# In-projections in pieces of 512 weight columns, and gate and up products with 512 moving columns, in a four-layer decoder trunk

## The chip, the cores and the metric

The kernel runs on one core of one Trainium2 chip. The metric is the device time of one execution in microseconds (us), the median of three runs. Six actors matter below: TensorE (PE, matmuls; PEld is its weight load, which runs beside it), VectorE (DVE), ScalarE (ACT), GpSimd (POOL), and SyncE (SP), which issues the DMA transfers. TensorE has two clock levels, 1.2 and 2.4 GHz; the profile shows which share of full speed it was granted.

## The reference, cut to what matters

Four layers over 256 positions of width 1024. Each layer is a token mixer with a memory attention beside it, one output projection, a normalisation, a gated feed-forward net (FFN) of width 2816, and a second normalisation. The mixer kinds are 0, 1, 2, 0: kind 0 picks keys by an indexer before it attends, kind 1 combines three dilated groups of heads, kind 2 comes down to causal attention at this length.

```
for i in range(4):                                  # x: 256 x 1024
    q, k, v, (qi, wi, ki), qm = split(x @ w_in[i])  # 768, 768, 768, (512, 8, 64 in kind 0), 256 columns
    q, k = rope(q), rope(k)                         # first 16 of each head's 64 columns turn; qi, ki too
    if kind == 0:  sel = top_64(sum_h wi * relu(qi_h . ki)); mix = attention(q, k, v, over sel)
    if kind == 1:  o_g, l_g = dilated(q_g, k_g, v) for g in 0..2; mix = sum_g softmax(l)_g * o_g
    if kind == 2:  mix = causal_attention(q, k, v)
    mk, mv = split(layer_norm(mem) @ w_mem_kv[i])
    mo = attention(qm, mk, mv)
    x = layer_norm(ALPHA * x + concat(mix, mo) @ w_out[i])
    g, u = split(x @ w_gate_up[i])                  # 2816 columns each
    x = layer_norm(ALPHA * x + (silu(g) * u) @ w_down[i])
```

## The kernel before, in words

**Products.** Every fp32 product is made as three passes. Each operand is split into a high part (`wh`, `xh`, `fth`) and a low part, the rest (`wl`, `xl`, `ftl`), and `mm3` issues high by high, low by high and high by low (L260, L261, L262). So each tile of a product is three matmuls.

**Weights.** The weights stream through the chip once. `weight_plan` lists pieces (`v`, `qk`, `qi`, `qm`, `mk`, `mv`, `out`, `gu`, `dn`) in order of use. Each piece is a few halves of 128 x 1024 floats (512 KB): a DMA issued by SP (L210) brings one into a `raw` buffer (4 of them), ACT casts the high part (L218), and DVE (L234) or POOL (L232, two instructions of 512 columns) subtracts for the low part. POOL takes three of four halves in the mixers and none in the FFN. Six buffers hold converted pairs (`NB = 6`).

**Forms of a product.** `a_mode` keeps the activations stationary and moves the weights: for each of 8 depth blocks three matmuls of as many columns as the piece is wide, once for each half of the positions (tb 0 and tb 1). The in-projection pieces use it: six pieces `qk` (one pair of heads each, 128 columns of q and 128 of k), three `v`, and for the indexer `qi` in 328 and 256 columns. `t_mode` keeps the weights stationary and moves the activations, 256 columns (all positions). The FFN's gate and up pieces (`gu`, 22 a layer, of which the first two use `a_mode`) and `qm` use it. The down and output projections move 512 weight columns.

**A gate and up piece.** `t_mode` leaves gate and up in one PSUM bank; `t_task` then runs silu on ACT (L1025), the product with up on DVE (L1027), the high part on ACT (L1029) and the low part on DVE (L1031). The plan of the FFN alternates two `gu` pieces with one `dn` piece, which uses products of the pair of `gu` pieces before the last one done and the first of that pair.

**A pair of heads.** A `qk` bank is copied to `nat` on ACT (L469), four small DVE operations turn its first columns (`rope`, L461 to L464), PE transposes it (L477), ACT and DVE copy q and k out (L571, L572), PE makes logits (L491), DVE masks them and takes their minimum (L502), ACT exponentiates, PE transposes the result (`turned`, L526) and multiplies with v (L543), DVE scales (L547), PE transposes again (L553), and the split (L269, L274) gives `fth` and `ftl` for the output projection.

**The dilated combine.** In layer 1 `dil_combine` adds the three groups' exponentials with weights: on DVE small operations on `st` tiles (L882 to L889), two scalings (L892) and four multiply-adds per half of the positions (L894; tiles `e`, 128 x 128 for tb 0, `E`, 128 x 256 for tb 1). There are two sets of heads (jp 0, jp 1) by two halves, so four combines. Before the change, the pieces of jp 0 come first and its combines are spawned after the third of them, in the middle of the in-projections; jp 1's at the end.

**Order.** PE runs in the order in which the program is written: a small scheduler written in Python (`tick`) places the steps of waiting tasks between groups of large matmuls. The other engines are ordered by a tile scheduler by priority. The memory's normalisation (two multiply-adds of 128 x 512 per half, L350 and L352, DVE) is a low-priority task of layer 0; PE transposes its result (L326).

## Time and profile before

| | |
|---|---|
| median of 3 runs | 1340.44 us (1339.45 to 1341.69) |
| profiled execution: time | 1339.27 us |
| profiled execution: span of the instructions | 1337.5 us |
| mean granted TensorE clock | 0.995 |
| PE busy | 1305.3 us, 98% of the span |
| DVE, ACT, POOL busy | 776.9, 651.3, 313.3 us |
| weights moved | 224.10 MB, 51.2% of the DMA engines' time |

A busy time is the sum of an engine's instructions on the profile. Matmuls overlap in the pipeline, so a matmul's duration is longer than the time to the next one's start; where the pace of PE counts, starts are compared.

### The profile page before, as it was taken

What the parts mean: (1) busy time and instruction counts of PE and PEld (TensorE: products, weight loads), DVE (VectorE), ACT (ScalarE), POOL (GpSimd) and SP (SyncE); (2) the same over time, 40 slices, a digit from 0 to 9 for tenths busy, and PEclk for the clock granted to TensorE, in tenths of its full rate; (3) what the DMA queues carried; (4) which work ended last, traced back from release to release, by engine and by line L of the source; (5) the groups of instructions that cost most, each with busy time, mean ns of one, the idle gap of its engine ahead of it and who ended that gap; (6) DMA issues with size and microseconds to landing.
All of it is one profiled execution on the core that took longest, in us unless ns stands there. A gap on an engine that the chain in (4) does not pass through costs nothing.

```text
span 1337.5 us, 23972 instructions
## 1 busy us (share of the span) xinstructions
PE 1305.3 (98%) x9370; PEld 1205.4 (90%) x9370; DVE 776.9 (58%) x1660; ACT 651.3 (49%) x1216; POOL 313.3 (23%) x277
## 2 busy tenths in 40 slices
PE   7899999999999999999999999999998999999997
PEld 5799899999999799999999989999987998899996
DVE  7845465555656874555474465555576755655555
ACT  5556454444465554444456545444445654444441
POOL 3543330000353440000054442000034443300000
PEclk9999999999999999999999999999999999999999
DMA  8443365556463356555554337656544333655551
GB/s 293 162 157 112 110 231 186 185 187 188 150 214 112 111 175 219 189 183 185 177 188 137 110 118 234 187 187 189 187 155 172 127 111 111 209 187 187 188 176 62
DMA packets 63186, 225.63 MB, mean 169 GB/s; under 512 B 7776, under 2 KB 7776, under 8 KB 63072
## 3 DMA queue, kind: packets, MB, share of 16 engines
q1 hardware_dynamic: 62784, 224.10, 51.2%
q8 instruction: 73, 1.20, 0.4%
q14 instruction: 41, 0.34, 0.1%
q10 hardware_dynamic: 288, 0.00, 0.0%
HBM read 223.02 MB, written 1.05 MB: 168 GB/s over the span
## 4 chain that ended last, share of the span: by engine, by line
PE 89%; DVE 5%; issue 2%; POOL 2%; DMA 1%; ACT 1%; SPq 0%; DVEq 0%; POOLq 0%; ACTq 0%
PE bank L260 27%; PE bank L262 26%; PE bank L261 26%; PE bank L491 3%; PE bank L543 3%; POOL wl L232 2%; PE bank L526 2%; DMA raw<-in_w 1%; PE bank L477 1%; DVE wl L234 1%; PE bank L326 1%; DVE E L894 1%; PE bank L553 1%; ACT wh L218 0%; DVE e L894 0%
## 5 line engine op out<-in xcount | busy, mean ns | idle before, releaser
L218 ACT CAST wh<-raw 128x1024 fp32r<-128x1024 f32 (+1 forms) x402 | 421.0, 1048 | 366.7 <-PE bank L261 179.3
L234 DVE TENSOR_TENSOR wl<-raw,wh 128x1024 fp32r<-128x1024 f32 (+1 forms) x294 | 379.3, 1291 | 296.0 <-ACT wh L218 294.9
L232 POOL TENSOR_TENSOR wl<-raw,wh 128x512 fp32r<-128x512 f32 x216 | 293.7, 1383 | 726.5 <-ACT wh L218 690.8
L260 PE MATMUL bank<-xh,wh 128*128 128x256 f32 x1344 | 381.7, 284 | 0.0
L262 PE MATMUL bank<-xh,wl 128*128 128x256 f32 x1344 | 380.3, 283 | 0.0
L261 PE MATMUL bank<-xl,wh 128*128 128x256 f32 x1344 | 380.3, 283 | 0.0
L260 PEld LDWEIGHTS bank<-xh,wh 128*128 128x128 f32 x1344 | 257.7, 192 | 2.8 <-issue 1.3
L261 PEld LDWEIGHTS bank<-xl,wh 128*128 128x128 f32 x1344 | 257.7, 192 | 1.2
L262 PEld LDWEIGHTS bank<-xh,wl 128*128 128x128 f32 x1344 | 257.7, 192 | 0.0
L260 PE MATMUL bank<-wh,xh 128*128 128x256 f32 (+1 forms) x768 | 231.4, 301 | 1.3 <-ACT xh L269 0.9
L261 PE MATMUL bank<-wl,xh 128*128 128x256 f32 (+1 forms) x768 | 219.5, 286 | 2.2 <-DVE wl L234 2.2
L262 PE MATMUL bank<-wh,xl 128*128 128x256 f32 (+1 forms) x768 | 219.5, 286 | 1.4 <-DVE xl L274 1.4
L260 PE MATMUL bank<-wh,fth 128*128 128x512 f32 x480 | 190.5, 397 | 0.4 <-ACT fth L269 0.4
L261 PE MATMUL bank<-wl,fth 128*128 128x512 f32 x480 | 187.4, 390 | 0.0
L262 PE MATMUL bank<-wh,ftl 128*128 128x512 f32 x480 | 187.3, 390 | 0.0
L260 PEld LDWEIGHTS bank<-wh,xh 128*128 128x128 f32 x768 | 147.6, 192 | 10.8 <-issue 6.4
L261 PEld LDWEIGHTS bank<-wl,xh 128*128 128x128 f32 x768 | 148.0, 193 | 2.6 <-DVE wl L234 2.6
L262 PEld LDWEIGHTS bank<-wh,xl 128*128 128x128 f32 x768 | 147.6, 192 | 1.8 <-DVE xl L274 1.8
L262 PEld LDWEIGHTS bank<-wh,ftl 128*128 128x128 f32 x480 | 90.1, 188 | 19.9 <-DVE ftl L274 0.4
L260 PEld LDWEIGHTS bank<-wh,fth 128*128 128x128 f32 x480 | 90.3, 188 | 18.8 <-issue 1.3
L261 PEld LDWEIGHTS bank<-wl,fth 128*128 128x128 f32 x480 | 90.4, 188 | 16.4
L1029 ACT CAST fth<-sil 128x256 fp32r<-128x256 f32 x80 | 32.5, 406 | 107.3 <-DVE sil L1027 107.3
(158 smaller groups left out, 1255.3 us busy)
## 6 DMA issues: line engine op xcount, KB each, us to landing
raw<-in_w SPq DMA_DIRECT2D x396, 512.0 KB, 4.2
lng<-in_ln_g SPq DMA_DIRECT2D x8, 512.0 KB, 5.5
lnb<-in_ln_b SPq DMA_DIRECT2D x8, 512.0 KB, 6.6
raw<-in_w SPq DMA_DIRECT2D x4, 492.0 KB, 4.9
x<-in_xT SPq DMA_DIRECT2D x2, 512.0 KB, 5.3
E<-in_mem SPq DMA_DIRECT2D x4, 256.0 KB, 6.0
x<-in_x SPq DMA_DIRECT2D x2, 512.0 KB, 5.8
out_x<-x SPq DMA_DIRECT2D x4, 256.0 KB, 2.1
```

The source lines that it names most:

```text
L218: self.nc.scalar.copy(c[0][:, 0:wd], self.raw[n][:, 0:wd])
L232: self.nc.gpsimd.tensor_tensor(lo[:, c], r[:, c], hi[:, c], op=OP.subtract)
L234: self.nc.vector.tensor_tensor(lo[:, 0:wd], r[:, 0:wd], hi[:, 0:wd], op=OP.subtract)
L260: mm(out, lhsT=ah, rhs=bh, start=first, stop=False)
L261: mm(out, lhsT=ah, rhs=bl, start=False, stop=False)
L262: mm(out, lhsT=al, rhs=bh, start=False, stop=last)
L326: nc.tensor.transpose(p[:, k], ys[half][:, k * 128:k * 128 + 128], self.ident)
L477: self.nc.tensor.transpose(p[:, c], n[:, c * 128:c * 128 + 128], self.ident)
L491: self.nc.tensor.matmul(bs[h][:, 0:nk], lhsT=q[r], rhs=k[r, 0:nk], start=True, stop=True)
L526: self.nc.tensor.transpose(p[:, sb, h], e[:, h, sb * 128:sb * 128 + 128], self.ident)
L543: nc.tensor.matmul(b[:, h * n:h * n + n], lhsT=pT[:, sb, h], rhs=vs[h][:, sb], start=sb == 0, stop=sb == nsb - 1)
L1029: nc.scalar.copy(fts[i][0], s)
```

## The change

The in-projection pieces get wider. Three `qk` pieces of 512 columns (two pairs of heads: 256 of q, 256 of k) take the place of six of 256; `v` becomes one piece of 512 and one of 256 (328 with the indexer's 72 columns in kind 0); the indexer's queries are one piece of 512. A bank of 512 columns is turned by one `rope` for 8 heads, in place, and copied by operations of twice the width. Two `nat` buffers of 512 columns stand in place of three of 256, the exponentials have six buffers of each size in place of three. The plan's order is written anew, and in layer 1 all four combines are spawned after the last in-projection piece.

The gate and up pieces that used `t_mode` use a new `wide_mode`: the activations' high and low parts lie side by side in one tile `x2`, so `wh` is loaded once and moves 512 columns (high by high and high by low at once, in two halves of a bank), then `wl` moves 256. Gate and up take a bank each, and `t_task` first adds the two halves: an ACT copy and a DVE addition for each, 128 x 256.

```diff
-        v = [("v", l, i) for i in range(3)]
-        qk = [("qk", l, i) for i in range(6)]
+        va, vb = ("v", l, 0), ("v", l, 1)
+        qk, qm = [("qk", l, i) for i in range(3)], ("qm", l, 0)
         if kind == 0:
-            qi, qm = [("qi", l, 0), ("qi", l, 1)], ("qm", l, 0)
-            if l:
-                plan += [*qi, v[0], qk[0], qm, qk[1], v[1], qk[2], qk[3], qk[4], v[2], qk[5]]
-            else:
-                plan += [*qi, v[0], qm, qk[0], qk[1], v[1], qk[2], qk[3], qk[4], qk[5], v[2]]
-                i = plan.index(MEM_AT)
-                plan[i:i] = [("mk", 0, 0), ("mv", 0, 0)]
+            plan += [vb, ("qi", l, 0), va]
+            plan += [qk[0], qm, qk[1], qk[2]] if l else [qm, qk[0], ("mk", 0, 0), ("mv", 0, 0), qk[1], qk[2]]
         elif kind == 1:
-            plan += [v[0], qk[0], ("qm", l, 0), qk[2], v[1], qk[4], qk[1], qk[3], qk[5], v[2]]
+            plan += [qk[0], va, qm, qk[1], qk[2], vb]
         else:
-            plan += [v[0], qk[0], ("qm", l, 0), qk[1], v[1], qk[2], qk[3], v[2], qk[4], qk[5]]
+            plan += [va, qk[0], qm, qk[1], qk[2], vb]
...
-    return 328 if piece[0] == "qi" and piece[2] == 0 else 256
+    what, l, i = piece
+    if what in ("qk", "qi") or what == "v" and i == 0:
+        return 512
+    return 328 if what == "v" and KINDS[l] == 0 else 256
...
-        self.nats = one([128, 256], "nat", 3)
-        self.qs = one([128, 128], "q", 6)
+        self.nats = one([128, 512], "nat", 2)
...
-        self.es = {128: one([128, 2, 128], "e", 3), 256: one([128, 2, 256], "E", 3)}
+        self.es = {128: one([128, 2, 128], "e", 6), 256: one([128, 2, 256], "E", 6)}
...
+        self.x2 = T([128, 8, 2, S], F32R, "x2")
+        self.xT = (self.x2[:, :, 0], self.x2[:, :, 1])
...
+    def wide_mode(self, key):
+        mm = self.nc.tensor.matmul
+        bs = [self.take(self.banks, "bank") for _ in range(2)]
+        for c in range(2):
+            for h in range(2):
+                w = self.half(key, h)
+                cs = [slice(k * 256 + c * 128, k * 256 + c * 128 + 128) for k in range(4)]
+                for k in range(4):
+                    mm(bs[c], lhsT=w[0][:, cs[k]], rhs=self.x2[:, 4 * h + k].rearrange("p a t -> p (a t)"),
+                       start=h == k == 0, stop=False)
+                for k in range(4):
+                    mm(bs[c][:, 0:S], lhsT=w[1][:, cs[k]], rhs=self.x2[:, 4 * h + k, 0], start=False, stop=h == 1 and k == 3)
+                if c:
+                    self.free_half(key, h)
+                if not (c and h):
+                    self.tick()
+        return bs
...
+        e = self.nc.vector
+        e.tensor_tensor(B, A, sb, op=OP.mult)
+        e.tensor_tensor(A, A, cb, op=OP.mult)
         e.tensor_tensor(d4[:, :, 0:8], A[:, :, 0], B[:, :, 1], op=OP.subtract)
         e.tensor_tensor(d4[:, :, 8:16], A[:, :, 1], B[:, :, 0], op=OP.add)
...
+        self.nc.scalar.copy(n, bank)
+        self.rope(n, bank, 8, tb, st)
...
+        self.nc.scalar.activation(q[tb], p[:, 0:2], AF.Copy, scale=SCALE)
+        self.nc.vector.tensor_copy(kb[:, :, tb * 128:tb * 128 + 128], p[:, 2:4])
...
+    def qk_ready(self, flags, tb, i):
+        while not (("k", 0) in flags and ("k", tb) in flags):
+            yield 1
+        if i:
+            yield W_PAIR
...
-        def combine(jp):
-            done[3 * jp] = [self.spawn(self.dil_combine(jp, tb, parts, v, mix)) for tb in range(2)]
...
+        if kind == 1:
+            for jp in range(2):
+                done[3 * jp] = [self.spawn(self.dil_combine(jp, tb, parts, mix)) for tb in range(2)]
...
-        def t_task(i, b, p):
+        def t_task(i, bs):
             s = yield from self.tk(self.sils)
-            nc.scalar.activation(s, p[:, 0], AF.Silu)
+            u = yield from self.tk(self.sils)
+            for d, b in ((s, bs[0]), (u, bs[1])):
+                nc.scalar.copy(d, b[:, S:2 * S])
+                nc.vector.tensor_tensor(d, b[:, 0:S], d, op=OP.add)
+                self.banks.put(b)
+            nc.scalar.activation(s, s, AF.Silu)
             yield 1
-            nc.vector.tensor_tensor(s, s, p[:, 1], op=OP.mult)
-            self.banks.put(b)
+            nc.vector.tensor_tensor(s, s, u, op=OP.mult)
+            self.sils.put(u)
...
-            b, p = self.t_mode(self.xT, ("gu", l, i))
+            bs = self.wide_mode(("gu", l, i))
             fts[i] = self.take(self.fts, "ft")
-            gut[i, 0] = gut[i, 1] = self.spawn(t_task(i, b, p))
+            gut[i, 0] = gut[i, 1] = self.spawn(t_task(i, bs))
...
+        elif what == "v" and i == 0:
+            a = col_piece(wi, (2 * MIXW, 512))
         elif what == "v":
-            a = col_piece(wi, (2 * MIXW + 256 * i, 256))
+            a = col_piece(wi, (2 * MIXW + 512, 256), *([] if KINDS[l] else [(3 * MIXW + 512, 72)]))
```

What the order of instructions shows, at three places. First PE inside the FFN, in one gate and up piece. Before, each depth block is three rows:

```order
L260 MATMUL bank_66<-xh,wh_85 128x256
L261 MATMUL bank_66<-xl,wh_85 128x256
L262 MATMUL bank_66<-xh,wl_86 128x256
L260 MATMUL bank_66<-xh,wh_85 128x256
L261 MATMUL bank_66<-xl,wh_85 128x256
```

and now (`x_150` is the tile `x2`, L976 a small transpose that belongs to another task):

```order
L315 MATMUL bank_65<-x_150,wh_77 128x512 x4
L318 MATMUL bank_65<-x_150,wl_78 128x256 x4
L315 MATMUL bank_65<-x_150,wh_79 128x512 x4
L318 MATMUL bank_65<-x_150,wl_80 128x256 x4
L976 MATMUL bank_70<-ident,sil_133 128x128
L315 MATMUL bank_66<-x_150,wh_77 128x512 x4
```

The same products stand in two rows of four where twelve stood: two matmuls of 256 columns became one of 512, and the third is unchanged.

Second, PE at the end of layer 1's mixer, where the combined exponentials of jp 1 (`e_98`, `E_101`) are transposed between matmuls of the output projection (`fth`, `ftl`). Before:

```order
L526 MATMUL bank_66<-ident,e_98 128x128 x2
L260 MATMUL bank_63<-wh_83,fth_127 128x512
L261 MATMUL bank_63<-wl_84,fth_127 128x512
L262 MATMUL bank_63<-wh_83,ftl_128 128x512
L260 MATMUL bank_69<-wh_83,fth_127 128x512
L261 MATMUL bank_69<-wl_84,fth_127 128x512
L262 MATMUL bank_69<-wh_83,ftl_128 128x512
L526 MATMUL bank_70<-ident,E_101 128x128 x4
L260 MATMUL bank_68<-wh_83,fth_127 128x512
```

and now (`e_94`, `E_100` belong to jp 0, `e_95`, `E_101` to jp 1; L541 is the transpose, L558 the product with v, L568 the last transpose):

```order
L258 MATMUL bank_67<-wh_79,ftl_127 128x512
L541 MATMUL bank_64<-ident,e_94 128x128 x2
L541 MATMUL bank_63<-ident,e_95 128x128 x2
L541 MATMUL bank_65<-ident,E_100 128x128 x4
L558 MATMUL bank_66<-v,pa_106 128x192 x2
L558 MATMUL bank_64<-v,pa_107 128x192 x2
L541 MATMUL bank_63<-ident,E_101 128x128 x4
L558 MATMUL bank_65<-v,pb_111 128x192 x4
L568 MATMUL bank_66<-ident,on_114 128x128 x3
L568 MATMUL bank_64<-ident,on_112 128x128 x3
L558 MATMUL bank_63<-v,pb_109 128x192 x4
L256 MATMUL bank_68<-wh_81,fth_128 128x512
```

On DVE, ahead of the transpose of `E_101`, now (L861 is the multiply-add, L859 the scaling, L849 to L856 the small operations):

```order
L856 RECIPROCAL st_140<-st_140 128x2
L861 SCALAR_TENSOR_TENSOR E_100<-E_102,st_140,E_100 128x256 x2
L861 SCALAR_TENSOR_TENSOR E_100<-E_104,st_140,E_100 128x256 x2
L849 TENSOR_TENSOR st_145<-st_145 128x2
L850 TENSOR_TENSOR st_145<-st_145 128x6
L853 TENSOR_TENSOR st_145<-st_145 128x6
L859 TENSOR_SCALAR E_101<-E_101,st_145 128x256
L854 TENSOR_TENSOR st_145<-st_145 128x2
L859 TENSOR_SCALAR E_101<-E_101,st_145 128x256
L855 TENSOR_TENSOR st_145<-st_145 128x2
L861 SCALAR_TENSOR_TENSOR E_101<-E_103,st_145,E_101 128x256
```

All four combines stand at the end of the mixer on DVE, and no matmul of a projection is left between their transposes on PE; before, two of the four stood in the middle of the in-projections.

Third, DVE in layer 0, around the end of the key selection (`sil_130` with L719 and L720 before, `sil_133` with L727 and L728 after). `E_100` and `E_101` are here the normalised memory. Before:

```order
L720 MATCH_REPLACE sil_130<-st_147,sil_130 128x256
L502 ISA bank_68,st_135<-bank_68,sel_173 128x128
L502 ISA st_135 128x1
L502 ISA bank_70,st_135<-bank_70,sel_173 128x128
L502 ISA st_135 128x1
L350 SCALAR_TENSOR_TENSOR E_101<-E_101,st_148,lng 128x512
L572 COPY k_133<-bank_66 128x128
L352 SCALAR_TENSOR_TENSOR E_100<-E_100,st_148,lnb 128x512
L352 SCALAR_TENSOR_TENSOR E_101<-E_101,st_148,lnb 128x512
L725 TENSOR_SCALAR sel_174<-sil_130 128x256
```

and now (the two L368, which are L352 before, stand some 40 rows earlier, among the first rounds of the selection):

```order
L451 CAST sil_134<-sil_132 128x256
L728 MATCH_REPLACE sil_133<-st_147,sil_133 128x256
L452 TENSOR_SCALAR dil_1308<-sil_134 128x256
L727 MAX st_147<-sil_133 128x8
L270 TENSOR_TENSOR ml<-bank_69,mh 128x4x128
L728 MATCH_REPLACE sil_133<-st_147,sil_133 128x256
L727 MAX st_147<-sil_133 128x8
L728 MATCH_REPLACE sil_133<-st_147,sil_133 128x256
L733 TENSOR_SCALAR sel_170<-sil_133 128x256
L475 TENSOR_TENSOR st_148<-bank_63,sin_242 128x128
L476 TENSOR_TENSOR bank_63<-bank_63,cos_241 128x8x16
```

The memory's normalisation moved ahead of the selection's rounds, and the `rope` of the first `qk` piece (L475, L476) stands behind them.

## Rows read from the trace of the kernel before

**Rows 1.** The page: busy time by engine, and the chain that ended last.

```profile
PE 1305.3 (98%) x9370; PEld 1205.4 (90%) x9370; DVE 776.9 (58%) x1660; ACT 651.3 (49%) x1216; POOL 313.3 (23%) x277
PE 89%; DVE 5%; issue 2%; POOL 2%; DMA 1%; ACT 1%; SPq 0%; DVEq 0%; POOLq 0%; ACTq 0%
```

**Rows 2.** Windows: PE, PEld, DVE, ACT, POOL busy (instructions); clock, DMA share, GB/s.

```profile
256.00:288.00 32.00, 32.00 (x226) 30.08 (x226) 16.50 (x19) 13.58 (x20) 0.00 (x0) 1.00 0.59 193
448.00:480.00 32.00, 29.82 (x155) 24.01 (x154) 24.37 (x56) 13.47 (x35) 14.99 (x12) 1.00 0.30 102
68.00:72.00 4.00, 4.00 (x21) 3.29 (x20) 3.90 (x17) 1.88 (x6) 0.74 (x2) 0.57 0.99 346
```

**Rows 3.** Timeline of PE in layer 2's FFN: start, duration, line, tiles.

```profile
844.27 0.28 PE L260 MATMUL bank<-xh,wh 128*128 128x256 f32 x1
...
855.66 0.28 PE L262 MATMUL bank<-xh,wl 128*128 128x256 f32 x1
855.78 0.40 PE L260 MATMUL bank<-wh,fth 128*128 128x512 f32 x1
...
856.71 0.39 PE L261 MATMUL bank<-wl,fth 128*128 128x512 f32 x1
...
861.25 0.28 PE L260 MATMUL bank<-xh,wh 128*128 128x256 f32 x1
...
861.72 0.28 PE L261 MATMUL bank<-xl,wh 128*128 128x256 f32 x1
```

**Rows 4.** Groups by line and shape: count, busy us, mean ns, idle before.

```profile
L218 ACT CAST wh<-raw 128x1024 fp32r<-128x1024 f32 x396 | 415.5, 1050 | 365.5 <-PE bank L261 179.3 <-PE bank L262 80.3 <-issue 76.5
...
L232 POOL TENSOR_TENSOR wl<-raw,wh 128x512 fp32r<-128x512 f32 x214 | 291.2, 1384 | 726.5 <-ACT wh L218 690.8 <-PE bank L477 15.4 <-PE bank L262 12.8
...
L1027 DVE TENSOR_TENSOR sil<-sil,bank 128x256 f32<-128x256 f32 x80 | 33.2, 415 | 0.0
...
L603 ACT COPY v<-bank 128x256 f32<-128x256 f32 x24 | 8.9, 373 | 10.1 <-PE bank L262 9.7
```

**Rows 5.** Timeline of DVE in the same FFN, the end of a piece's chain.

```profile
859.02 0.42 DVE L1031 TENSOR_TENSOR ftl<-sil,fth 128x256 fp32r<-128x256 f32 x1 [0.47 <-ACT fth L1029]
```

**Rows 6.** Timeline of PE in layer 0, its longest wait after the start.

```profile
67.50 0.66 PE L326 MATMUL bank<-ident,E 128*128 128x128 f32 x4 [3.46 <-DVE E L352]
```

**Rows 7.** Timeline of DVE in layer 0, its last work before that wait ends.

```profile
66.70 1.40 DVE L352 SCALAR_TENSOR_TENSOR E<-E,st,lnb 128x512 f32<-128x512 f32 x2
```

**Rows 8.** Timeline of PE at the end of layer 1's mixer.

```profile
454.49 0.70 PE L491 MATMUL bank<-k,q 64*128 64x256 f32 x4 [0.68 <-DVE k L572]
...
465.31 0.55 PE L526 MATMUL bank<-ident,E 128*128 128x128 f32 x3 [1.01 <-DVE E L894]
```

**Rows 9.** Timeline of DVE there: combine of tb 0, masks, combine of tb 1.

```profile
454.36 0.15 DVE L886 TENSOR_TENSOR st<-st 128x6 f32<-128x6 f32 x1
...
454.96 0.34 DVE L894 SCALAR_TENSOR_TENSOR e<-e,st,e 128x128 f32<-128x128 f32 x1
...
455.30 2.86 DVE L894 SCALAR_TENSOR_TENSOR e<-e,st,e 128x128 f32<-128x128 f32 x3
458.08 0.42 DVE L502 CUSTOM_DVE_ANT_0 bank<-bank,dil 128x256 f32<-128x256 f32 x1
...
459.17 0.17 DVE L883 TENSOR_TENSOR st<-st 128x6 f32<-128x6 f32 x1
...
460.50 0.48 DVE L894 SCALAR_TENSOR_TENSOR E<-E,st,E 128x256 f32<-128x256 f32 x1
...
460.97 4.28 DVE L894 SCALAR_TENSOR_TENSOR E<-E,st,E 128x256 f32<-128x256 f32 x3
```

**Rows 10.** Timeline of POOL there.

```profile
455.16 2.59 POOL L232 TENSOR_TENSOR wl<-raw,wh 128x512 fp32r<-128x512 f32 x2 [1.55 <-ACT wh L218]
460.73 5.67 POOL L232 TENSOR_TENSOR wl<-raw,wh 128x512 fp32r<-128x512 f32 x4 [2.98 <-ACT wh L218]
```

**Rows 11.** Timeline of PE in layer 3, its longest wait there.

```profile
1019.67 0.46 PE L491 MATMUL bank<-k,qi 64*128 64x128 f32 x2 [3.74 <-DVE bank L462]
```

More of the change, by code (lines that the diff above doesn't have):

```diff
@@ L695, in select_task @@
         for pr in range(4):
[L696 removed]
+            while tb not in qi:
                 yield 1
             bs = yield from self.tk2()
[L699 removed]
+            L = self.logits(bs, self.qi[tb][:, pr], kb[:, 0], nk)
             for r in L:
```

263 lines of the change are left out of this document (96 added, 167 removed).

## The prediction

> **What bounds the kernel now.** I read the page's busy times first: PE is busy for 1305.3 of 1337.5 us, and the chain that ended last runs through PE for 89% of the span and through DVE for 5% [rows 1]. So what counts is the pace of PE's matmuls, and the places where PE waits. The windows show both kinds of stretch. In an FFN PE is busy for all 32 us of a window while DVE works 16.50 and ACT 13.58, and POOL nothing (first row of [rows 2]): there only PE's own pace matters. At the end of layer 1's mixer PE has gaps (29.82 of 32), DVE is at 24.37 and POOL at 14.99 (second row of [rows 2]).
>
> The pace comes from starts in the timeline [rows 3]. From 844.27 to 855.66 lie 95 intervals of 256-column matmuls: 11.39 / 95 = 0.1199 us each. From 855.78 to 861.25 lie 24 of 512 columns: 5.47 / 24 = 0.2279. Two matmuls of 256 cost 0.2398, one of 512 costs 0.2279: **a merge saves 0.0119 us** at full clock.
>
> PE's longest waits outside the start of the program are three. In layer 0 it waits 3.46 us for the memory's normalisation [rows 6], which ends on DVE at 68.10 [rows 7]. In layer 3 it waits 3.74 us for DVE's rope of the indexer's queries [rows 11]. At the end of layer 1's mixer it waits 0.68 and 1.01 us, the second for a dilated combine [rows 8]. A long wait costs a second time: in the 4 us after the one in layer 0 the granted clock is 0.57 (third row of [rows 2]), which is half speed for 3.4 us, so 1.7 us of work lost.
>
> **The change part by part.** The sum is made against the profiled execution, 1339.3 us; the median of the three runs is 1.2 us above it.
>
> *Gate and up.* 20 pieces in each of 4 layers use the wide form; the order shows 32 merges into 16 in each, so 16 x 80 = 1280 merges. At the steady pace they save 1280 x 0.0119 = 15.2 us. But now four 512-column matmuls alternate with four of 256, so I take the first ones after a switch: from 855.78 to 856.71, four of 512, 0.93 us; from 861.25 to 861.72, four of 256, 0.47 us [rows 3]. That is 1.40 for a group against 12 x 0.1199 = 1.44; four groups a piece save 0.15, and 80 pieces **12.2 us**. If each of the 320 groups loses another 0.015 at its two switches, 7.4 are left; the upper bound is 16, the steady pace with a little.
> The price is two ACT copies and two DVE additions of 128 x 256 from PSUM a piece. Nearest rows: 373 ns for the ACT copy, 415 for the DVE operation [rows 4]. In 32 us lie fewer than four pieces, so DVE goes from 16.5 to some 19.5 and ACT from 13.6 to 16.4 of 32 [rows 2]: neither becomes the bound. The piece's chain grows by at most 2 x (0.373 + 0.415) = 1.6 us. Before, it ended at 859.44 [rows 5], 3.7 us after the piece's last matmul at 855.66; it becomes 5.3. What needs it first, the second half of a `dn` piece, comes one `gu` piece (5.6 us) and 12 matmuls of 512 (2.7 us) later, 8.3 in all. 3 us of cover are left, so I cost this at nothing. If the chain took 9 us, each of some 40 `dn` pieces would wait 0.7.
>
> *In-projections.* The order shows 864 merges: 576 in `qk`, 192 in `v`, 96 in `qi`. At 0.0119 that is 10.3 us. Small matmuls interrupt these streams, and a part runs below full clock; I take **9 us**, bounds 7 and 11. DVE's rope becomes half as many operations of twice the width, ACT's and DVE's copies likewise: less busy time on both, mostly beside PE, counted at nothing.
>
> *End of layer 1's mixer.* Before, combine tb 0 takes 454.36 to 458.08, 3.7 us, and combine tb 1 459.17 to 465.25, 6.1 us [rows 9]. Most of it is the multiply-adds. The first of each kind takes 0.34 and 0.48, the next three 2.86 and 4.28, so 0.95 and 1.43 each, and those run while POOL works (455.16 to 457.75, 460.73 to 466.40) [rows 10]. The Trainium skill, "SBUF — State Buffer", section "SBUF: two separate sides", says that GpSimd and a VectorE operation with two SBUF inputs exclude each other on one port pair; these rows agree, 0.48 against 1.43 us.
> After the change two combines of each kind and two pairs of masks (0.9 us each, 458.08 to 458.98 where the small operations begin) stand in a row on DVE. Beside POOL that is 2 x (3.72 + 6.08) + 1.8 = 21.4 us. Without POOL the slow multiply-adds drop by 1.84 and 2.84 a combine, which gives 12.0. PE has, from the logits that feed the first of it to the transposes that need it, 24 matmuls of 256 (2.9), 24 of 512 (5.5) and two groups of logits (1.3): 9.6 us of work. So PE waits 2.4 to 11.8 us. POOL is busy in 47% of this window [rows 2]; that share of the way gives 6.8. Behind it the chain product with v, scaling, transpose, split is now bare, since no projection matmul stands between: about 1.5 us of DVE and ACT. The lower clock after a long wait adds 1.7, as in layer 0. The two old waits here go, 0.68 + 1.01 = 1.7 [rows 8]. Together 6.8 + 1.5 + 1.7 - 1.7 = **+8.3 us**; bounds +2 (no contention, no clock loss) and +15.
>
> *Layer 0.* DVE's two multiply-adds for the memory move ahead of most of the selection, so the 3.46 us wait and its clock loss go: -5.2. In turn the rope of the first `qk` piece now stands behind the selection's last rounds, and PE's transpose of it behind that. No row shows this wait; the nearest is layer 3's 3.74, where rope stands behind other DVE work [rows 11]. I take 2.7, so **-2.5** net; bounds -6 (nothing new) and +4 (a longer wait with its own clock loss).
>
> *Layer 3 and the weights.* Layer 3's wait has the same cause after the change (a rope behind DVE work): 0, with -5 if it goes. The weights are the same bytes in the same halves. A 512-column piece keeps its four halves until tb 1 has passed, so four of six buffers are held: the third and fourth half of the next piece can be cast only when tb 1's pass frees one, at +1.36 and +2.72 us of it (6 x 0.2279 each). A cast takes 1.05 and POOL's two instructions 2.77 [rows 4], so the last is converted at 6.5 to 8 us; it is needed at +8.2 and +9.5 (tb 1's remainder and the next piece's first pass). 1.5 to 3 us of cover: 0, with +5 for some late ones.
>
> The sum: 1339.3 - 12.2 - 9 + 8.3 - 2.5 = **1323.9 us**.
>
> **The rivals.** *More gain.* The combines run mostly without POOL, and the waits in layers 0 and 3 go with their clock loss. For it: POOL's rows have gaps, and the plan of halves is new. Against it: POOL's busy half of that window. 1339.3 - 12.2 - 9 + 2 - 6 - 5 = 1309; 1307 to 1315.
>
> *A dear tail.* The combines run beside POOL throughout, and the chain behind pays again: +15 to +18 at the end of layer 1, and layer 0 gives nothing: 1339.3 - 21.2 + 15 to 18 = 1333 to 1336, up to 1339.
>
> *Slower: late weights in the wide pieces.* The cover of 1.5 to 3 us is used up, as ACT and DVE share their time with rope, softmax and selection, and each of the 18 wide in-projection pieces (5, 4, 4, 5 by layer) waits for its last halves. It decides from 23.7 - 8.3 = 15.4 us of gain eaten, about 0.9 us a piece, if all else goes as forecast; at 1.4 a piece it gives 1323.9 + 25.2 = 1349. Against it: POOL has room (23% busy), and it holds 2% of the chain that ended last [rows 1].
>
> *No change: merging saves nearly nothing.* If the 0.0119 us a merge is not there, because the fixed cost of a matmul hides in rows that I compared across stages (weights moving against activations moving), the two first terms shrink; with a fifth of them left, 1339.3 - 4.2 + 8.3 - 2.5 = 1340.9. Against it: the two cadences lie side by side in one FFN at clock 1.00. The Trainium skill, "TensorE: Matmul & The Clock Gate", section "Back-to-back issue gap", is the rule for it: 262 cycles for 256 columns and 518 for 512, so a merge saves 6 cycles, 2.5 ns at 2.4 GHz, and all 2144 of them an estimated 5.4 us. The trace shows 0.1199 and 0.2279, both longer than that and 0.0119 apart, so I go by the trace.
>
> **How the numbers follow.** About 0.2%, 2.7 us, is what a measurement of this kernel can tell from no change. The forecast case, 1315 to 1331, gets 0.72; more gain 0.13; the dear tail 0.07; late weights 0.04; no merge gain 0.02; 0.02 is left for what I have not seen. The range 1311 to 1336 takes in the forecast, half of "more gain" and most of the dear tail. Faster by over 0.2% (under 1337.8): 0.72 + 0.13 + 0.06 = 0.91. Within it: 0.04, from the dear tail's end and no merge gain. Slower: 0.05.
>
> **What would show it.** PE's count falls by 2144; in an FFN two `gu` and a `dn` take 16.98 us now (96 x 0.1199 + 24 x 0.2279) and about 16.68 after, without waits; DVE's busy time rises from 777 to about 825 and ACT's from 651 to about 700. At the end of layer 1 the transposes of `E` wait for the multiply-add, by 5 us or more in sum. In layer 0 the transposes of the memory no longer wait, and those of the first `qk` piece's `nat` do, by 2 to 3. I am wrong if FFN windows show PE waiting for an addition, if a period there stays near 17, if PE's weight loads in the in-projections wait for `wl` at the start of a second half, or if the end of layer 1 costs nothing.

## The result, and the profile after

The changed kernel takes 1322.36 us (median of 4 runs, 1319.02 to 1324.36) against 1341.0 for the kernel before: ratio 0.986, 95% interval 0.9834 to 0.9886. The forecast was 1323.9. Its profiled execution, the longest of the four, took 1324.36 us with a span of 1321.4, 16.1 less than the span before. The page, engines first, then the chain that ended last:

```profile
PE 1289.8 (98%) x7226; PEld 1093.2 (83%) x7226; DVE 822.6 (62%) x1684; ACT 695.6 (53%) x1312; POOL 316.4 (24%) x277
PE 88%; DVE 5%; issue 2%; DMA 2%; POOL 2%; ACT 1%; SPq 0%; DVEq 0%; POOLq 0%; ACTq 0%
```

PE issues 9370 - 7226 = 2144 matmuls fewer; DVE and ACT rise to 823 and 696 us, as forecast (825, 700). PE is still busy for 98%. Inside an FFN PE still never pauses, though DVE and ACT have more to do than in [rows 2]; behind the waits its clock is low. Windows, columns as in [rows 2]:

```profile
256.00:288.00 32.00, 32.00 (x170) 27.44 (x169) 19.56 (x27) 16.31 (x28) 0.00 (x0) 1.00 0.61 190
...
448.00:452.00 4.00, 1.95 (x6) 1.43 (x7) 3.69 (x15) 2.00 (x5) 0.37 (x1) 0.52 0.44 131
452.00:456.00 4.00, 4.00 (x18) 3.91 (x18) 2.43 (x7) 0.37 (x1) 0.00 (x0) 0.63 0.00 0
...
680.00:684.00 4.00, 4.00 (x15) 3.31 (x16) 2.64 (x3) 0.59 (x1) 0.96 (x1) 0.57 0.91 272
```

PE's longest waits after the start of the program, the work behind the third of them, and a piece of an FFN (in square brackets the wait and what ended it):

```profile
29.93 0.48 PE L683 MATMUL bank<-ident,kd 128*128 128x128 f32 x1 [3.86 <-DVE kd L678]
...
73.51 0.63 PE L492 MATMUL bank<-ident,nat 128*128 128x128 f32 x4 [1.86 <-DVE nat L478]
...
449.19 1.21 PE L541 MATMUL bank<-ident,E 128*128 128x128 f32 x4 [3.83 <-DVE E L861]
451.25 2.93 PE L558 MATMUL bank<-v,pa 128*128 128x192 f32 x8 [0.86 <-ACT pa L542]
453.98 1.06 PE L541 MATMUL bank<-ident,E 128*128 128x128 f32 x4
...
679.90 0.81 PE L342 MATMUL bank<-ident,x 128*128 128x128 f32 x4 [2.59 <-DVE x L368]
...
845.60 1.09 PE L315 MATMUL bank<-x,wh 128*128 128x512 f32 x4
846.52 0.64 PE L318 MATMUL bank<-x,wl 128*128 128x256 f32 x4
847.00 1.09 PE L315 MATMUL bank<-x,wh 128*128 128x512 f32 x4
```

A group of the wide form takes 847.00 - 845.60 = 1.40 us, the forecast's figure (0.92 for four of 512, 0.48 for four of 256). The waits of [rows 6] and [rows 11] are gone. In their place PE waits for the indexer's key (3.86; before, 0.76 us for it and 3.25 for a rope stood near there), for the first `qk` rope (1.86, forecast 2 to 3), for the combined exponentials in layer 1 (3.83), and at the start of layer 2 for the normalisation of x (2.59; 0.55 before).

To see where the time went I cut the span at starts of matmuls in PE's timeline: a layer's 360 matmuls with `fth` or `ftl` are 96 of the output projection and 264 of the down projection. "Mixer" runs from the last down matmul of the layer before to the last output matmul, "FFN" from there to the layer's last down matmul.

| us | layer 0 | layer 1 | layer 2 | layer 3 | sum |
|---|---|---|---|---|---|
| mixer before | 167.3 | 119.3 | 120.5 | 146.1 | 553.2 |
| mixer after | 163.3 | 120.8 | 122.2 | 143.4 | 549.7 |
| FFN before | 194.6 | 194.6 | 194.6 | 192.4 | 776.3 |
| FFN after | 191.7 | 191.7 | 191.7 | 188.6 | 763.8 |

The FFNs give 12.5 us, 2.9 in each layer and another 0.9 in the last one, where an old wait for the low part of x is gone. The mixers give 3.5, but not layer by layer as forecast: in these two executions layers 1 and 2 became longer.

How far a stage moves though nothing in it changes can be read from the experiments below, since many of them leave a mixer with the same instructions in the same order on PE, DVE, ACT and POOL. Among such profiled executions of the changed kernel's mixers layer 0 took 162.3 to 164.2 us (seven of them), layer 1 120.3 to 121.9 (four), layer 2 119.1 to 122.8 (six) and layer 3 141.2 to 143.4 (six). So a mixer's difference of a microsecond or two between two single executions is not yet an effect. The FFN stretches agree to 0.02 us.

### The profile page after: what moved, and what is told of

Its sections match the earlier page's. It is cut to its first block, busy times and chain, and to the rows that moved or that the text cites. A ratio compares the mean times of both kernels' runs of the same rounds, so it can differ in the third digit from the quotient of the medians.

```text
span 1321.4 us, 19878 instructions
## 1 busy us (share of the span) xinstructions
PE 1289.8 (98%) x7226; PEld 1093.2 (83%) x7226; DVE 822.6 (62%) x1684; ACT 695.6 (53%) x1312; POOL 316.4 (24%) x277
## 4 chain that ended last, share of the span: by engine, by line
PE 88%; DVE 5%; issue 2%; DMA 2%; POOL 2%; ACT 1%; SPq 0%; DVEq 0%; POOLq 0%; ACTq 0%
PE bank L315 22%; PE bank L256 15%; PE bank L258 14%; PE bank L257 14%; PE bank L318 11%; PE bank L558 3%; PE bank L506 3%; PE bank L541 1%; POOL wl L228 1%; DMA raw<-in_w 1%; PE bank L492 1%; DVE wl L230 1%; PE bank L342 1%; DVE sil L728 1%; PE bank L568 1%
## 5 line engine op out<-in xcount | busy, mean ns | idle before, releaser
L315 PE MATMUL bank<-x,wh 128*128 128x512 f32 x1280 | 349.5, 394 | 0.0
L315 PEld LDWEIGHTS bank<-x,wh 128*128 128x128 f32 x1280 | 221.1, 189 | 31.3
L318 PEld LDWEIGHTS bank<-x,wl 128*128 128x128 f32 x1280 | 196.3, 189 | 26.9
L318 PE MATMUL bank<-x,wl 128*128 128x256 f32 x1280 | 203.7, 281 | 0.0
L256 PE MATMUL bank<-wh,x 128*128 128x512 f32 (+2 forms) x480 | 182.6, 380 | 2.5 <-ACT wh L214 1.3
L257 PE MATMUL bank<-wl,x 128*128 128x512 f32 (+2 forms) x480 | 170.9, 356 | 2.1 <-DVE wl L230 2.1
L258 PE MATMUL bank<-wh,x 128*128 128x512 f32 (+2 forms) x480 | 171.1, 356 | 0.5 <-DVE x L270 0.5
L256 PEld LDWEIGHTS bank<-wh,x 128*128 128x128 f32 x480 | 92.5, 193 | 24.1 <-issue 9.6
L258 PEld LDWEIGHTS bank<-wh,x 128*128 128x128 f32 x480 | 92.4, 192 | 13.8 <-DVE x L270 1.0
L257 PEld LDWEIGHTS bank<-wl,x 128*128 128x128 f32 x480 | 92.8, 193 | 10.8 <-DVE wl L230 2.6
L986 ACT COPY sil<-bank 128x256 f32<-128x256 f32 x160 | 58.5, 365 | 61.5 <-PE bank L318 61.5
L987 DVE TENSOR_TENSOR sil<-bank,sil 128x256 f32<-128x256 f32 x160 | 67.1, 419 | 30.7 <-ACT sil L986 30.7
```

The source lines that it names most:

```text
L256: mm(out, lhsT=ah, rhs=bh, start=first, stop=False)
L257: mm(out, lhsT=ah, rhs=bl, start=False, stop=False)
L258: mm(out, lhsT=al, rhs=bh, start=False, stop=last)
L315: mm(bs[c], lhsT=w[0][:, cs[k]], rhs=self.x2[:, 4 * h + k].rearrange("p a t -> p (a t)"), start=h == k == 0, stop=False)
L318: mm(bs[c][:, 0:S], lhsT=w[1][:, cs[k]], rhs=self.x2[:, 4 * h + k, 0], start=False, stop=h == 1 and k == 3)
L986: nc.scalar.copy(d, b[:, S:2 * S])
```

## The experiments

Ratios are against the kernel before, run on the same chip; its median lay at 1340.6 to 1341.0 in all of these. "Mixer" and "FFN" are as in the table.

**Each half of the change alone.** e1: the kernel before with the new gate and up pieces (`x2`, `wide_mode` and the additions of `t_task` with them).

```diff
...
-            b, p = self.t_mode(self.xT, ("gu", l, i))
+            bs = self.wide_mode(("gu", l, i))
...
-            gut[i, 0] = gut[i, 1] = self.spawn(t_task(i, b, p))
+            gut[i, 0] = gut[i, 1] = self.spawn(t_task(i, bs))
```

> The kernel before with the wide gate and up pieces alone; the in-projections stay at 256 columns. Theory (a merge of two 256-column matmuls into one of 512 saves about 0.012 us, less what the switches between 512 and 256 columns cost, and the additions are hidden): each FFN's stretch from its first wide piece to its last matmul falls from 175.2 to about 172.3 us, the program by 11.7, to 1329 (ratio 0.991). Rival (merging saves only the few ns that the skill's gap rule gives, and the FFN's gain came with other parts of the change): FFN stretch at 174.4 or more, program 1337 or more (ratio 0.998).

Measured: 1327.26 us, ratio 0.9903 (0.9882 to 0.9923). Between first and last down matmul a layer takes 166.45 us in place of 169.24, what it takes in the changed kernel; with the piece ahead of the first down matmul that is 2.92 a layer. The theory stands.

e2: the changed kernel with the old gate and up pieces (the same edit backwards).

> The changed kernel with the old gate and up pieces (256 moving columns, one bank, no additions). Theory (the two halves of the change add up): the FFN stretches are back at 175.2 us each, the program is 11.7 us slower than the whole change, 1334 (ratio to the kernel before 0.995), and the mixers keep the waits of the changed kernel: about 4 us for the combined exponentials in layer 1, none for the memory's normalisation in layer 0. Rival (the extra work on DVE and ACT in the FFN delays the mixers behind it, such as the wait at the start of layer 2): that wait of 2.7 us in layer 2 shrinks to 0.7 and the program comes to 1330 or less.

Measured: 1330.64, ratio 0.9931 (0.9907 to 0.9955); the down stretch is back at 169.24. The in-projections alone give 10 us, more than the 7 left for them in the whole change. Layer 2's wait is 2.00 us here, not 0.7, so the rival's reason is not it. In the medians the two halves do not simply add up: 13.5 + 10.1 is 5 us more than the 18.6 of the whole. But the mixers of e2 have the changed kernel's instructions in the same order, and their sum is 544.9 us in this profile against 549.7 in that of the changed kernel: 4.8 us that no difference of instructions explains.

**Is it the merging?** e3 issues each 512-column matmul of a gate or up piece as two of 256.

```diff
-                for k in range(4):
-                    mm(bs[c], lhsT=w[0][:, cs[k]], rhs=self.x2[:, 4 * h + k].rearrange("p a t -> p (a t)"),
-                       start=h == k == 0, stop=False)
...
+                    for k in range(4):
+                        mm(bs[c][:, a * S:a * S + S], lhsT=w[0][:, cs[k]], rhs=self.x2[:, 4 * h + k, a],
+                           start=h == k == 0, stop=bool(a and h == 1 and k == 3))
```

(with a loop over a, the two halves of x2, around the loop over h)

> The changed kernel, but in the gate and up pieces each matmul of 512 columns is issued as two of 256 (high by high for the whole depth, then high by low), with the same two banks and the same additions. Theory (the gain is the merging itself): 1280 matmuls more at 0.0119 us, FFN stretch from 172.3 to about 175.5 to 176.1 us in each layer, program 13 to 15 us slower than the changed kernel, 1335 to 1338 (ratio to the kernel before 0.997). Rival (the gain comes from something else in the new form, such as the order of passes or the separate banks): FFN stretch stays within 0.5 us of 172.3 and the program at 1322 to 1324.

Measured: 1331.13, ratio 0.9929 (0.9908 to 0.995). The down stretch is 169.24, exactly that of the kernel before, although two additions, two copies and a second bank a piece are still there. So the FFN's gain is the merging, all of it, and the additions cost nothing. I had expected 3.2 to 3.8 a layer and it is 2.9: the steady pace of [rows 3] would give 3.8, the switches between the two widths take 0.9. The program is 8.8 us slower than the change, not 11.7: in its profiled execution the mixers, whose instructions are the changed kernel's, are 3.6 us shorter, 2.2 of it in layer 3.

e9 does the same to the in-projections.

```diff
...
+                cols = [slice(0, 512)] if k == 0 else [slice(0, 256), slice(256, 512)]
+                for s in cols:
+                    mm(p[:, s], lhsT=x[0], rhs=y[0][:, s], start=k == 0, stop=False)
+                for s in [slice(0, 256), slice(256, 512)]:
+                    mm(p[:, s], lhsT=x[0], rhs=y[1][:, s], start=False, stop=False)
+                for s in [slice(0, 256), slice(256, 512)]:
+                    mm(p[:, s], lhsT=x[1], rhs=y[0][:, s], start=False, stop=k == 7 and s.start > 0)
```

> The changed kernel with the 512-column matmuls of the in-projections issued as two of 256 columns (828 of the 864; the first of each accumulation stays whole), everything else as in the change: same pieces, buffers, rope, order. Theory (the in-projections' gain is the merging, 0.012 us each): 828 matmuls more cost 9.9 us, of which the waits at the starts of layers may take back 1 to 3; program 1329 to 1332 (ratio to the kernel before 0.992). Rival (their gain comes from fewer and wider operations on DVE and ACT or from the new order): program 1326 or less.

Measured: 1323.36, ratio 0.9867 (0.9853 to 0.9882): no different from the change. The theory missed. PE's timeline of this kernel:

```profile
701.39 0.40 PE L293 MATMUL bank<-wh,x 128*128 128x256 f32 x2
701.63 0.40 PE L289 MATMUL bank<-wh,x 128*128 128x256 f32 x2
701.87 0.40 PE L291 MATMUL bank<-wl,x 128*128 128x256 f32 x2
...
73.41 0.63 PE L502 MATMUL bank<-ident,nat 128*128 128x128 f32 x4 [0.47 <-DVE nat L488]
```

and of the changed kernel at the same place:

```profile
701.28 0.40 PE L256 MATMUL bank<-wh,x 128*128 128x512 f32 x1
701.51 0.39 PE L257 MATMUL bank<-wl,x 128*128 128x512 f32 x1
701.74 0.39 PE L258 MATMUL bank<-wh,x 128*128 128x512 f32 x1
```

Pairs start 0.24 us apart, matmuls of 512 columns 0.23. Over all neighbours of the in-projections in the two timelines (starts under 0.27 us apart) the means are 0.2387 and 0.2301: a merge saves about 0.0086 here, and 828 of them 7 us. The 0.0119 of the prediction comes only where no small matmul interrupts (69 intervals from 684.27 to 699.92 in the changed kernel: 0.2268 each).

The program does not pay these 7 us, because some waits shrink when PE comes later. At the `qk` rope in layer 0 PE waits 1.85 to 1.87 us in each of nine profiled kernels with merged pieces, and 0.47 here. In layer 3 a `nat` (0.60 to 0.69) and a k (1.09 to 1.13) are waited for in each of them, for 0.26 and 0.56 here. By layer the mixers are 163.9, 123.1, 120.3 and 142.2: layer 1 is 1.2 to 2.8 longer than in the executions with merged pieces, where 184 merges are worth 1.6 at this pace, and layers 0, 2 and 3 lie inside their spread. Layer 2's wait for the normalisation (0.55 here) hangs on a transfer, as shown below, and says nothing on the merging.

**The end of layer 1.** In the changed kernel, DVE and POOL there:

```profile
437.16 1.40 DVE L861 SCALAR_TENSOR_TENSOR e<-e,st,e 128x128 f32<-128x128 f32 x1
...
439.64 1.45 DVE L861 SCALAR_TENSOR_TENSOR e<-e,st,e 128x128 f32<-128x128 f32 x1
...
446.28 3.16 DVE L861 SCALAR_TENSOR_TENSOR E<-E,st,E 128x256 f32<-128x256 f32 x4
...
451.20 1.26 DVE L861 SCALAR_TENSOR_TENSOR E<-E,st,E 128x256 f32<-128x256 f32 x3
```

```profile
437.08 5.14 POOL L228 TENSOR_TENSOR wl<-raw,wh 128x512 fp32r<-128x512 f32 x4 [6.76 <-ACT wh L214]
445.71 2.66 POOL L228 TENSOR_TENSOR wl<-raw,wh 128x512 fp32r<-128x512 f32 x2 [3.48 <-ACT wh L214]
```

Two of the sixteen multiply-adds last 1.4 us where the others of this width take 0.35, and the first two of the four at 446.28 are slow too (0.97 and 1.48, where the others take 0.47); all four overlap POOL's work. Together they lose 3.7 us. The last four run without POOL and three of them take 1.26 together. The forecast had 47% of 2 x (1.84 + 2.84), 4.4 us: the contention is somewhat smaller, not by much. What is smaller by far is the wait. PE waits 3.83 us for the first `E` alone. The second `E`'s combine ends at 452.46, while PE is at the product with v (L558, from 451.25), and its transposes at 453.98 wait for nothing. e7 takes POOL out of the output projection's weights in layer 1.

```diff
+        if self.plan[self.hv[n][0]][:2] == ("out", 1):
+            turn = (0, 1)
```

> The changed kernel with no low parts on POOL for layer 1's output projection (DVE makes them). Theory (a multiply-add with two SBUF inputs runs slower only beside POOL): the 16 multiply-adds of the combines last 0.26 to 0.48 us each, none over 1 us; DVE gains 4 us there and pays 1.2 us for each of some three low parts, so the wait for E at its transposes falls from 3.8 to 2 to 3.5 us. Rival (they are slow by themselves at some addresses, or beside ACT or DMA): several still last 1.2 us or more.

Measured, in one execution: 1317.39 us. Its groups by line and shape, and PE's waits there:

```profile
L863 DVE SCALAR_TENSOR_TENSOR E<-E,st,E 128x256 f32<-128x256 f32 x8 | 3.5, 475 | 0.0
L863 DVE SCALAR_TENSOR_TENSOR e<-e,st,e 128x128 f32<-128x128 f32 x8 | 2.6, 342 | 0.0
```

```profile
446.66 0.85 PE L543 MATMUL bank<-ident,E 128*128 128x128 f32 x4 [0.81 <-ACT wh L214]
...
450.60 0.94 PE L543 MATMUL bank<-ident,E 128*128 128x128 f32 x4 [1.78 <-DVE E L863]
```

Means of 475 and 342 ns where the change has 661 and 618 (L861 there), and all sixteen between 0.33 and 0.48 us: the theory stands. The waits at the transposes of `E` are 0.81 (put down to a cast on ACT) and 1.78. Layer 1's mixer takes 118.4, 2.4 less than in the profiled execution of the change and 1.9 less than in the shortest of the four with that kernel's layer 1.

e4 gives the combines cover instead: both v pieces behind the last `qk` piece.

```diff
-            plan += [qk[0], va, qm, qk[1], qk[2], vb]
+            plan += [qk[0], qk[1], qm, qk[2], va, vb]
```

> The changed kernel with layer 1's pieces in the order qk0, qk1, qm, qk2, va, vb, so that 17 us of v pieces stand behind the last qk piece where 6 us stood. Theory (the wait for the combined exponentials is DVE work that lacks cover on PE): the wait of 3.8 us at the transposes of E, the 0.9 behind it and the slow clock after them go, and the program falls by 5 to 7 us, to 1316 (ratio to the kernel before 0.982). Rival (DVE is short in all of this stretch, or the wait only moves, to the scaling or the last transposes): less than 2 us gained, another wait of 3 us or more in layer 1.

Measured: 1313.22, ratio 0.9799 (0.9779 to 0.982). Layer 1's mixer falls from 120.8 to 115.2, 5.7 us, and the waits for the combines are gone. One of the two left, each about 1 us:

```profile
438.18 0.33 PE L568 MATMUL bank<-ident,on 128*128 128x128 f32 x1 [0.90 <-DVE on L562]
```

So the theory stands. The program gained 9.1, more than layer 1 did: layer 2's mixer was 3.1 shorter in this run, layer 3's 1.1. Both have the same instructions as in the changed kernel, so these 4.2 us are not cover for the combines.

**The start of layer 2.** The chain there in the changed kernel, ACT first, then DVE:

```profile
675.50 1.05 ACT L214 CAST wh<-raw 128x1024 fp32r<-128x1024 f32 x1 [4.62 <-DMA raw<-in_w]
```

```profile
676.58 1.22 DVE L230 TENSOR_TENSOR wl<-raw,wh 128x1024 fp32r<-128x1024 f32 x1 [3.14 <-ACT wh L214]
677.72 0.15 DVE L352 TENSOR_SCALAR st<-st 128x1 f32<-128x1 f32 x1
677.78 1.41 DVE L366 SCALAR_TENSOR_TENSOR bank<-bank,st,lng 128x512 f32<-128x512 f32 x2
679.10 1.40 DVE L368 SCALAR_TENSOR_TENSOR x<-bank,st,lnb 128x512 f32<-128x512 f32 x2
```

DVE idles for 3.14 us with the normalisation (L352, L366, L368) ready behind a low part whose cast waits for a transfer. That transfer, the second of four issued within 3.5 us, landed 6.3 us after its issue here, 4.4 in the kernel before. How much PE waits goes by that landing. The same matmul in the kernel before (4.4 us), in e4 (4.8) and in e8 (6.8), the last two with the changed kernel's instructions in this mixer:

```profile
686.35 0.66 PE L326 MATMUL bank<-ident,x 128*128 128x128 f32 x4 [0.55 <-DVE x L352]
```

```profile
673.63 0.66 PE L342 MATMUL bank<-ident,x 128*128 128x128 f32 x4 [1.04 <-DVE x L368]
```

```profile
679.91 0.66 PE L342 MATMUL bank<-ident,x 128*128 128x128 f32 x4 [3.04 <-DVE x L368]
```

e5 raises the normalisation's priority.

```diff
-PRIO_CV, PRIO_XT, PRIO_LN, PRIO_MEM = 110, 60, 0, 150
+PRIO_CV, PRIO_XT, PRIO_LN, PRIO_MEM = 110, 60, 60, 150
```

> The changed kernel with the normalisation of a layer's result ahead of the weights' low parts in DVE's order (priority offset 60 in place of 0). Theory (the new waits at the start of layers 2 and 3, 1.9 and 1.2 us beyond those before, come because a low part whose cast waits for a late DMA stands on DVE ahead of the normalisation that PE needs next): those waits for the multiply-add of the normalisation fall under 0.5 us each, the slow clock after them goes, and the program gains 3 to 7 us, to 1315 to 1319 (ratio to the kernel before 0.981 to 0.984). Rival (PE lacks cover there, one piece of 512 columns, whatever stands on DVE): the waits stay above 1.5 us, and the program is at 1320 to 1324.

Measured: 1319.99, ratio 0.9844 (0.9825 to 0.9863). DVE at the same place, 4 us earlier in the layer and with the low part behind the normalisation:

```profile
673.74 1.40 DVE L366 SCALAR_TENSOR_TENSOR bank<-bank,st,lng 128x512 f32<-128x512 f32 x2
675.05 1.40 DVE L368 SCALAR_TENSOR_TENSOR x<-bank,st,lnb 128x512 f32<-128x512 f32 x2
676.37 1.21 DVE L230 TENSOR_TENSOR wl<-raw,wh 128x1024 fp32r<-128x1024 f32 x1
```

PE no longer waits there, and layer 2's mixer takes 117.84 us here, in e6 and in e10 alike: 4.4 less than in the profiled execution of the change, 1.3 less than in e4. So the cause of the wait is shown, and its price lies between 1.3 and 4.9 us by the landing of the transfer. The program gained only 2.4, a difference that the two intervals cover, and missed the forecast by 1 us: in layer 3 a wait of 1.73 us for the indexer's key took the old one's place, and at the start of the last FFN a low part that now stands behind the normalisation came 1.48 us late.

e11 makes the same edit in the kernel before.

> The kernel before with the normalisation first on DVE. Theory (the change made this order dearer, since less work of PE covers the normalisation; before, the waits there were 0.7 to 1.4 us a layer): 1 to 3 us gained at most, 1338 to 1340 (ratio 0.998 to 1.0). Rival (the order costs the same in both kernels): 4 us or more gained, in layer 2 as much as the 4.4 us in the changed kernel.

Measured: 1339.09, ratio 0.9988 (0.9977 to 0.9999); layer 2's mixer 0.7 shorter. That is the theory's range, and the rival's 4 us are not there. But that the change made this order dearer is not shown: the kernel before was profiled with a landing of 4.4 us and a wait of 0.55, and the changed kernel waits 1.04 with one of 4.8 (e4). In the medians the edit gains 1.5 us in one kernel and 2.4 in the other.

e6 has the edits of e4 and e5 together.

> The changed kernel with both the v pieces of layer 1 last and the normalisation first on DVE. If the two waits are separate and both are as the theories say, 1313.2 less 3 to 5 us: 1308 to 1310 (ratio to the kernel before 0.976). If the normalisation's place tells nothing, 1313 (0.980).

Measured: 1314.36, ratio 0.9806 (0.9789 to 0.9822), no better than e4, where 1308 to 1310 was forecast: layer 1 keeps its gain (114.5) and layer 2 its own (117.8), but the FFNs give 2.4 us back, 1.7 of it in layer 3 for the late low part.

**The start of layer 0.** DVE and POOL ahead of the 3.86 us wait for the key, in the changed kernel:

```profile
24.75 1.19 DVE L676 COPY kd<-kn 128x64 f32<-128x64 f32 x1
...
27.17 1.19 DVE L476 TENSOR_TENSOR kn<-kn,cos 128x16 f32<-128x16 f32 x1
```

```profile
23.34 6.20 POOL L228 TENSOR_TENSOR wl<-raw,wh 128x512 fp32r<-128x512 f32 x5
```

e8 lets POOL begin two halves later.

```diff
-N_WARM, W_MEM, N_START = 14, 4, 7
+N_WARM, W_MEM, N_START = 14, 4, 9
```

> The changed kernel with POOL's first low part two halves later (the ninth half in place of the seventh). Theory (the 4 us wait in layer 0 at the transpose of the indexer's key comes from six tiny DVE operations that last 1.2 us each beside POOL instead of 0.2): they take under 0.3 us, the wait falls under 2 us and its slow clock shrinks, program 2 to 5 us faster than the changed kernel, 1318 to 1320 (ratio to the kernel before 0.984). Rival (DVE is full there, the two low parts of 1.2 us take the place): the wait stays at 3 us or more, program within 1 us of 1322.

Measured: 1321.56, ratio 0.9852 (0.9826 to 0.9878). The same lines of this kernel:

```profile
25.20 0.19 DVE L676 COPY kd<-kn 128x64 f32<-128x64 f32 x1
...
25.51 0.18 DVE L476 TENSOR_TENSOR kn<-kn,cos 128x16 f32<-128x16 f32 x1
```

So these operations take 0.2 us alone and 1.2 beside POOL. Neither forecast came: the wait falls only to 2.73 (the last copy to `kd` still meets POOL), and the program's gain is too small to tell. Layer 0's mixer took 161.8, and 160.3 in e10 with the same instructions, below the 162.3 to 164.2 of the changed kernel's.

**The parts together, and the merging once more.** e10 is e4 with the normalisation first only behind an FFN, and with e8's later POOL.

```diff
...
-            out.append(self.spawn(self.residual(tb, accs, last)))
+            out.append(self.spawn(self.residual(tb, accs, last, 60 if what == 'dn' else 0)))
...
-        with self.shift(-PRIO_LN):
+        with self.shift(-by):
```

> The changed kernel with layer 1's v pieces last, the normalisation first on DVE only after an FFN (not ahead of one, where the look at both together showed low parts coming late), and POOL's first low part two halves later. If each gives what its own run showed in its stage (5.7 us in layer 1; 1 to 4 in layers 2 and 3; 1.5 in layer 0): 1309 to 1312 (ratio to the kernel before 0.977). If the waits only move on: 1313 to 1315, as with the v pieces alone.

Measured: 1310.09, ratio 0.9771 (0.9756 to 0.9785), as forecast and 12 us under the change. Its mixers: 160.3, 114.5, 117.8, 144.0.

e12 is e10 with the edit of e9.

> The version with v last in layer 1, the normalisation first after an FFN and POOL later, with the 512-column matmuls of the in-projections again issued as two of 256 (828 of 864). Theory (in the changed kernel the merges' gain of 9.9 us was eaten by waits on DVE that a faster PE only reaches sooner; layers 1 and 2, where those waits are gone here, show it): layers 1 and 2 each 2.0 to 2.4 us longer than in that version, layers 0 and 3, which still have waits, 0 to 2; program 1314 to 1318 (ratio to the kernel before 0.981). Rival (merging in the in-projections is worth nothing, whatever waits stand there): layers 1 and 2 within 0.7 us, program 1310 to 1312 (ratio 0.977).

Measured: 1308.83, ratio 0.9768 (0.975 to 0.9787): again no slower, and under both forecasts. By layer: 158.7, 115.9, 119.5, 142.4. Layers 1 and 2, free of long waits, took 114.45 and 117.84 in e10 and, with the same instructions, in e6; here they take 1.45 and 1.70 more. That is what 184 split matmuls cost at the pace of these two streams: starts of 512 columns lie 0.2307 and 0.2294 us apart in e10, pairs 0.2389 and 0.2387 here, so 184 x 0.0082 = 1.5 and 184 x 0.0093 = 1.7. There the theory holds.

In layers 0 and 3 the 230 split matmuls cost nothing that shows; both are 1.6 us shorter than in e10. As in e9 the rope's wait in layer 0 shrinks (1.85 to 0.48) and the two of layer 3 (0.62 and 1.09 to 0.28 and 0.57). The rest of the difference is not shown to come from the split. Layer 3 takes 142.4 in e6 too, which has e10's instructions there. In layer 0 the two executions part before the first split matmul. Windows of e10, where PE waits 2.80 us for the key, with the last copy to `kd`:

```profile
12.00:16.00 4.00, 3.81 (x25) 3.81 (x26) 3.83 (x19) 2.21 (x8) 0.21 (x1) 1.00 0.77 249
24.00:28.00 4.00, 1.20 (x6) 0.66 (x6) 3.52 (x9) 1.44 (x2) 1.44 (x2) 0.95 0.99 346
28.00:32.00 4.00, 4.00 (x12) 3.26 (x13) 3.97 (x11) 0.27 (x1) 2.05 (x2) 0.62 1.02 412
```

```profile
26.62 1.25 DVE L678 COPY kd<-kd 128x64 f32<-128x64 f32 x1
```

and of e12, where it waits 0.49:

```profile
12.00:16.00 4.00, 3.82 (x16) 3.82 (x17) 3.09 (x15) 1.17 (x5) 0.00 (x0) 0.63 0.69 241
24.00:28.00 4.00, 3.51 (x29) 3.26 (x28) 3.77 (x11) 1.55 (x3) 0.00 (x0) 1.00 1.02 270
28.00:32.00 4.00, 4.00 (x36) 4.00 (x35) 3.77 (x8) 0.84 (x3) 3.17 (x3) 1.00 1.03 411
```

```profile
27.22 0.18 DVE L688 COPY kd<-kd 128x64 f32<-128x64 f32 x1
```

Both executions have a stretch at low clock, e10 behind the wait (0.62), e12 ahead of it (0.63 in the first window). So e12 reaches its first in-projection matmul of 512 columns at 19.51 and e10 at 17.96. The copy of the key meets POOL's work in e10 (from 26.57) and not in e12 (from 28.16). The split matmuls delay PE by only 0.3 us more up to the wait (26.95 - 19.51 against 25.13 - 17.96).

## Why the prediction was right, point by point

*Gate and up, -12.2: right.* -11.7 measured, twice (e1, e3). The group of 1.40 us, read from the first matmuls after a switch, was the right row; the steady pace would have said 15.2. (The working's own rows give 320 x (1.439 - 1.40) = 12.4, and 3.8 us where it has 3.7 for the end of a piece's chain; neither matters.) By the rule of the Trainium skill ("TensorE: Matmul & The Clock Gate", "Back-to-back issue gap") 320 merges would save an estimated 0.8 us a layer; the runs show 2.9, so here the measurement decides. The additions are hidden, as argued: L986 and L987 cost 58.5 and 67.1 us of ACT and DVE, and no time on PE.

*In-projections, -9: the saving is there, but too large, and it was let through to the end.* The term took 0.0119 us a merge from an FFN, where long rows of one width follow each other. Between the small matmuls of a mixer a merge saves 0.0086, so 864 are worth 7.4 us, near the lower bound of 7. And undoing them costs the program nothing that shows (e9, e12). The step that failed is "bounds 7 and 11": I let the saving run through in all four layers. In layers 1 and 2 it does, where no wait stands behind it (e12 against e10); in layers 0 and 3 a wait on DVE stands a few us behind, which a faster PE only meets sooner. What the new pieces do give (e2: 10 us) goes with the waits that went: 3.46 us in layer 0 and 3.74 in layer 3, each with a low clock behind it (granted 0.57 and 0.58 in 68:72 and 1020:1024 of the kernel before). No run separates the wider pieces from the new order of the plan that came with them.

*End of layer 1, +8.3: right in kind, too large.* Layer 1 became 1.5 us longer (2.6 in e8, whose instructions there are the same), with merges worth 1.7, so the end cost 3 to 4. The step that was mis-sized is the wait of 6.8, which put all four combines in a row ahead of the transposes. PE waits 3.83 us, for the first `E`; the second `E`'s combine lies beside PE's product with v. The sign "5 us or more in sum" did not come. The share beside POOL was nearly right (4.4 us of slow-down taken, 3.7 met), the chain behind cost 0.86 in place of 1.5, and the lower clock 3.4 us of work in place of 1.7 (granted 0.52 and 0.63 in 448:452 and 452:456). With the old waits gone (0.68, 1.01 and one of 1.37 for a k) that leaves about 5, so 1 us or more of this account stays open. Cover (e4) and POOL (e7) both move it as the step said. Without POOL beside them the multiply-adds take 475 and 342 ns, with it 661 and 618 in the mean (e7). The Trainium skill, "SBUF — State Buffer", section "SBUF: two separate sides", says that a VectorE operation with two SBUF inputs and a GpSimd operation that reads SBUF exclude each other for a whole instruction; e7 agrees.

*Layer 0, -2.5: right in kind.* The memory's wait went, the rope's came (1.86 against 2.7); the layer gained 4.0 in all, where this term and its share of the -9 made 5.0.

*Layer 2, not in the sum.* It became 1.7 us longer in the profiled execution and 0.3 longer in the mean of the six with these instructions, where the merges are worth 1.7. I had not read the starts of the layers: the wait of 0.55 there rested on a transfer's landing, and DVE's order made it 1.04 to 3.04 by that landing (e4, e8), 2.59 in the profiled execution with a granted clock of 0.57 behind it. e5 takes it away.

*Layer 3, 0: two errors that cancel.* Its 3.74 us wait went, which I had put at -5 in the bounds, and smaller ones came (1.86 for the normalisation, 1.13 and 0.60).

So the forecast of 1323.9 met 1322.36 in part by luck: the end of layer 1 was put 4 to 5 us too dear, layer 2 was 2 to 4 us dearer than put, and the merges in the in-projections were put 1.6 us too high and hardly came through in layers 0 and 3. Of the rivals, the late weights did not come (no wait for a second half's low part behind the start of the program). Merging without gain is refuted by e3 for the FFN; in the in-projections the pace refutes it too, though the program shows little of it.

What stays open: why the transfer at the start of layer 2 lands between 4.4 and 6.8 us after its issue, also in kernels with the same instructions there; and what the new order of the plan is worth without the wider pieces.

## What to carry to other kernels

A saving on the busiest engine counts only in stretches where that engine waits for nothing further on; read the next wait behind each edit, not the engine's share of the span. Price a wider instruction by the starts around a switch between widths, not by its steady pace. Look in the order of a helping engine for work that is ready but stands behind a transfer: one priority took 1.3 to 4.9 us off a mixer here, whose merges are worth 1.7. And before a microsecond in one stage is called an effect, look at that stage in other executions of the same instructions.
